# Which engine forms the second parts of the weights outside the middle of the MLP

## The chip, the cores and the metric

The kernel runs on one core of a Trainium2 chip. Its engines are named as the profile names them: PE is TensorE with the matmuls, PEld its loading of weights, DVE is VectorE, ACT is ScalarE, POOL is GpSimd and SP is SyncE, which issues most transfers. The metric is the device time of one execution in microseconds (us); the median of several executions is compared.

## What is computed

Two layers of an encoder over 256 tokens of width 1024, in float32. Each layer does, in short:

```python
h = rmsnorm(x, norm_mix_pre)
proj = h @ w_in                      # q, k, v of A; pool input; q, k, v of C; three gates
ya = global attention, 8 heads       # branch A
yb = centred average pooling, minus identity, mapped by w_pool   # branch B
yc = neighbourhood attention         # branch C
merged = sum(sigmoid(gate_i + b_i) * (y_i @ w_branch[i]) for i in range(3))
x = x + rmsnorm(merged @ w_out, norm_mix_post)
h = rmsnorm(x, norm_ffn_pre)
up = conv over 3 tokens(h @ w_up)    # 2 x 2816 columns: val and gate
x = x + rmsnorm((gelu(gate) * val) @ w_down, norm_ffn_post)
```

## The kernel before

All weights come as one list of 264 chunks of 128 x 1024 float32 numbers (`CHUNKS`), 132 for each layer, in the order in which TensorE takes them. In one layer these are the first columns of w_in (24 chunks), then in six steps of gates and branches two chunks of w_branch and four of w_in each (with the first of w_out's eight in the last step), the rest of w_out, eight chunks of w_up for the first four blocks of 128 columns of both halves, and then pieces of w_up (two chunks each) with one chunk of w_down behind each from the sixth on. The last six chunks of w_down (`TAIL_D`) and the last five of w_out (`TAIL_O`) are tails of their own.

Each weight is used as a sum of two parts. For half a chunk (512 columns) ScalarE copies `raw` to `hi` in the type fp32r, and then the second part is formed, `lo` = `raw` - `hi`. Each product is three matmuls (lines 196 to 198): hi with hi, hi with lo and lo with hi. Activations are split the same way (`split_from`, lines 203 to 207), by ScalarE and VectorE.

The function `split(c, h)` does this for half h of chunk c, and line 160 chooses the engine of the second part. Of every five chunks the one with `c % PN == 1` (PN is 5) goes to GpSimd, with an exception: the chunks of w_in ahead of column 2816, where the gates begin. All others go to VectorE. The chunks run ahead of TensorE: up to six are split before they are used (NSPL), in six buffers each of `hi` and `lo`, and five `raw` buffers are loaded ahead (NRAW). `feed` calls `split` at a priority that is 100 behind the place in the program (LATER), while what stands in `urgent()` is 400 ahead. A scheduler turns the priorities into one fixed order for each engine when the kernel is built; each engine then runs its own list in order, and waits where an operand is missing.

Where one part of a layer ends and the next begins (`boundary`), the 256 tokens are taken as two halves t of 128. `tail` multiplies the last chunks for t = 0 first and then for t = 1. As soon as the banks of a half are done, `residual` forms the norm of them: squares on ScalarE (line 223), their sum on VectorE (line 225), the power -0.5 on GpSimd (`st`, line 215), two products with the gain on VectorE (`big`, line 259) and two with the norm, added to x (line 262). `norm_h` does the same for the next norm of x: lines 223, 225 and 215 and two products `xn` (`big`, line 242). TensorE then turns these (line 247), and the turned tile is split into `hThi` on ScalarE (line 203) and `hTlo` on VectorE (line 204). The next weights are multiplied with it, again for t = 0 first. Behind w_out this is `turned`: six chunks of w_up for t = 0, then the rest of the norm of t = 1, then these chunks for t = 1. There are three such boundaries: behind w_out in either layer, and behind w_down in the first.

GpSimd does little else: the powers of line 215, parts of the rotation of branch A (line 372), the rotation's tables, and the DMAs of line 638.

Of the kernel before, what the change touches and what calls it, by code (L numbers as in the profile page):

```python
# [21 lines left out]
NF = 22  # L22
EPS = 1e-6
CH = 1024
PN, LATER = 5, 100
NRAW, NSPL = 5, 6
NY = 20
TAIL_O, TAIL_D, LAG = 5, 6, 5
# [6 lines left out]
def chunk_list():  # L35

    out = []
    for l in range(L):
        def wide(name, i, c0, n):
            per = CH // n  # L40
            for k in range(0, 8, per):
                out.append((name, l, i, k, per, c0, n))
        wide("w_in", 0, 512, 256)
        wide("w_in", 0, 0, 512)
        for f in range(4):
            wide("w_in", 0, 768 + 128 * f, 128)
        for f in range(8):
            wide("w_in", 0, 1280 + 128 * f, 128)
        wide("w_in", 0, 2304, 512)
        for i in (1, 0, 2):  # L50
            for c in range(2):
                for k in (0, 2):
                    out.append(("w_branch", l, i, k, 2, 512 * c, 512))
                if i == 2 and c == 1:
                    out.append(("w_out", l, 0, 0, 1, 0, 1024))
                wide("w_in", 0, 2816 + 1024 * i + 512 * c, 512)
        for d in range(1, 8 - TAIL_O):
            out.append(("w_out", l, 0, d, 1, 0, 1024))
        for d in range(8 - TAIL_O, 8):
            out.append(("w_out", l, 0, d, 1, 0, 1024))  # L60
        wide("w_up", 0, 0, 128 * NT)
        wide("w_up", 0, 128 * NF, 128 * NT)
        for f in range(NT, NF):
            wide("w_up", 0, 128 * f, 128)
            wide("w_up", 0, 128 * (NF + f), 128)
            if 0 <= f - LAG < NF - TAIL_D:
                out.append(("w_down", l, 0, f - LAG, 1, 0, 1024))
        for f in range(NF - TAIL_D, NF):
            out.append(("w_down", l, 0, f, 1, 0, 1024))
    return out  # L70


CHUNKS = chunk_list()
# [3 lines left out]
def encoder(ctx: ExitStack, tc: tile.TileContext, x, norms, wall, bgate, gqk, wpool, pscale,  # L77
# [66 lines left out]
    def feed_dma(upto=len(CHUNKS)):  # L144
        while cur["dma"] < upto and cur["dma"] < cur["lo"] + NRAW:
            c = cur["dma"]
            raw[c] = sb.tile([128, CH], FT, name="raw", bufs=NRAW)
            nc.sync.dma_start(raw[c], wall[c])
            cur["dma"] += 1

    def split(c, h):

        if h == 0:
            hi[c] = sb.tile([128, CH], FR, name="hi", bufs=NSPL)
            lo[c] = sb.tile([128, CH], FR, name="lo", bufs=NSPL)
        z = slice(h * CH // 2, (h + 1) * CH // 2)
        act.activation(hi[c][:, z], raw[c][:, z], AF.Copy)  # L157

        lean = c % PN == 1 and (CHUNKS[c][0] != "w_in" or CHUNKS[c][5] >= 2816)
        (pool if lean else dve).tensor_tensor(lo[c][:, z], raw[c][:, z], hi[c][:, z], op=OP.subtract)  # L160
        if h == 1:
            del raw[c]
            cur["lo"] += 1
            feed_dma()

    def feed(upto=len(CHUNKS)):

        at = tc.cur_priority
        tc.cur_priority = at + LATER
        while cur["lo"] < upto and cur["lo"] < min(cur["used"] + NSPL, cur["dma"]):  # L170
            c = cur["lo"]
            for h in range(2):
                split(c, h)
        tc.cur_priority = at
# [152 lines left out]
    with tc.issue_after(par["xn"].ins):  # L327
        split(0, 0)
    drive(entry[0])
    with tc.issue_after(par["hi"].ins), tc.issue_after(par["lo"].ins):  # L330
        split(0, 1)
# [8 lines left out]
    for l in range(L):  # L340
# [468 lines left out]
        for f in range(NT, NF):  # L809
# [3 lines left out]
            if f < 2 * NT:  # L813
                q = psbank()
                for z in range(2):
                    for t in range(2):
                        c = 512 * z + 128 * (f - NT)
# [105 lines left out]
```

## Time and profile before

| what | value |
|---|---|
| median of 3 runs | 837.64 us (836.85 to 838.1) |
| the profiled execution | 837.28 us, of which its span is 835.5 us |
| PE busy | 806.2 us |
| DVE busy | 597.0 us |
| ACT busy | 501.7 us |
| POOL busy | 182.5 us |
| second parts on DVE | 440, 307.0 us |
| second parts on POOL | 88, 122.7 us |

The rest of the profiled execution's time, 1.8 us, lies around its span. The busy times are those of one execution and of the whole span. Stages have different limits, so a change in one stage is read from that stage. An engine's idle time that is shown before an instruction is what it stood still, with the instruction or transfer that it waited for behind the arrow.

### The profile page before, as it was taken

The page shows a single profiled execution, that of the slowest core. Times are in us where ns is not written, and L with a number is a line of the kernel's source. Part 1 is how long each engine was busy: PE and PEld are TensorE (multiplying, and loading weights), DVE is VectorE, ACT ScalarE, POOL GpSimd, SP SyncE. Part 2 cuts the span into 40 slices and gives each one's busy share as a digit, 9 for nine tenths or more (in the row PEclk, how much of TensorE's full clock was granted, in tenths as well). Part 3 has the DMA queues.
Part 4 walks back from the last instruction along what each step waited for, and adds up shares of the span by engine and source line. Part 5 has one row for each costly group of instructions (what it writes and reads, how often), then busy time and mean ns, then how long its engine had stood idle before and what let it go on. Part 6 is the DMA issues. An engine that isn't in the chain of part 4 may idle for free.

```text
span 835.5 us, 13700 instructions
## 1 busy us (share of the span) xinstructions
PE 806.2 (96%) x5012; PEld 707.2 (85%) x5012; DVE 597.0 (71%) x1101; ACT 501.7 (60%) x1068; POOL 182.5 (22%) x183
## 2 busy tenths in 40 slices
PE   4989999999999999999999899999998999999997
PEld 4888788888779999999889887888887899999995
DVE  4799475676677976766689964777667598667664
ACT  5478565455658756566565865654545677565661
POOL 2421422122122111212122015112212211212120
PEclk9999999999999999999999999999999999999999
DMA  7947557655565765565355545456654655556531
GB/s 269 336 159 217 164 176 230 199 183 170 193 218 183 206 195 182 185 191 182 124 199 175 176 155 153 164 181 205 230 179 139 209 175 195 186 184 184 192 101 50
DMA packets 44867, 154.42 MB, mean 185 GB/s; under 512 B 6017, under 2 KB 6273, under 8 KB 44545
## 3 DMA queue, kind: packets, MB, share of 16 engines
q1 hardware_dynamic: 43776, 151.46, 55.9%
q0 software_dynamic: 1024, 2.10, 0.9%
q8 instruction: 39, 0.64, 0.3%
q14 instruction: 28, 0.22, 0.1%
HBM read 150.39 MB, written 1.05 MB: 181 GB/s over the span
## 4 chain that ended last, share of the span: by engine, by line
PE 81%; DVE 10%; issue 2%; ACT 2%; POOL 2%; DMA 1%; SPq 0%; DVEq 0%; POOLq 0%; ACTq 0%
PE ps L196 26%; PE ps L197 25%; PE ps L198 25%; DVE lo L160 3%; POOL st L215 2%; DVE big L242 1%; DMA x<-in_x 1%; DVE big L379 1%; PE ps L481 1%; ACT hi L157 1%; PE ps L471 1%; DVE x L262 1%; PE ps L530 1%; PE ps L497 1%; PE ps L596 0%
## 5 line engine op out<-in xcount | busy, mean ns | idle before, releaser
L157 ACT ACTIVATE hi<-raw 128x512 fp32r<-128x512 f32 x528 | 310.9, 624 | 115.3 <-PE ps L197 40.1
L160 DVE TENSOR_TENSOR lo<-raw,hi 128x512 fp32r<-128x512 f32 x440 | 307.0, 723 | 72.9 <-ACT hi L157 71.0
L160 POOL TENSOR_TENSOR lo<-raw,hi 128x512 fp32r<-128x512 f32 x88 | 122.7, 1414 | 510.4 <-ACT hi L157 499.7
L196 PE MATMUL ps<-hThi,hi 128*128 128x256 f32 x768 | 219.0, 285 | 0.0
L198 PE MATMUL ps<-hThi,lo 128*128 128x256 f32 x768 | 218.1, 284 | 0.0
L197 PE MATMUL ps<-hTlo,hi 128*128 128x256 f32 x768 | 217.9, 284 | 0.0
L196 PEld LDWEIGHTS ps<-hThi,hi 128*128 128x128 f32 x768 | 147.9, 193 | 2.2 <-issue 0.8
L197 PEld LDWEIGHTS ps<-hTlo,hi 128*128 128x128 f32 x768 | 147.9, 193 | 1.4
L198 PEld LDWEIGHTS ps<-hThi,lo 128*128 128x128 f32 x768 | 147.8, 192 | 0.1
L196 PE MATMUL ps<-hi,hThi 128*128 128x512 f32 (+1 forms) x352 | 136.0, 388 | 1.2 <-ACT hi L157 0.9
L198 PE MATMUL ps<-hi,hTlo 128*128 128x512 f32 (+1 forms) x352 | 134.4, 382 | 0.9 <-DVE hTlo L204 0.9
L197 PE MATMUL ps<-lo,hThi 128*128 128x512 f32 (+1 forms) x352 | 134.6, 383 | 0.3 <-DVE lo L160 0.2
L196 PE MATMUL ps<-hi,y 128*128 128x512 f32 x272 | 107.3, 394 | 0.0
L197 PE MATMUL ps<-lo,y 128*128 128x512 f32 x272 | 106.4, 391 | 0.0
L198 PE MATMUL ps<-hi,y 128*128 128x512 f32 x272 | 105.9, 389 | 0.0
L196 PEld LDWEIGHTS ps<-hi,hThi 128*128 128x128 f32 x352 | 66.4, 189 | 15.4 <-ACT hi L157 1.1
L198 PEld LDWEIGHTS ps<-hi,hTlo 128*128 128x128 f32 x352 | 66.4, 189 | 14.6 <-DVE hTlo L204 2.3
L197 PEld LDWEIGHTS ps<-lo,hThi 128*128 128x128 f32 x352 | 66.4, 189 | 14.1 <-DVE lo L160 2.1
L799 ACT ACTIVATE w<-ps,cvp 128x256 f32<-128x256 f32 x88 | 48.3, 557 | 35.0 <-DVE w L801 35.0
L800 DVE SCALAR_TENSOR_TENSOR w<-ps,cvp,w 128x255 f32<-128x255 f32 x88 | 41.8, 480 | 28.6 <-ACT w L799 28.5
L196 PEld LDWEIGHTS ps<-hi,y 128*128 128x128 f32 x272 | 51.2, 188 | 11.0 <-issue 1.1
L198 PEld LDWEIGHTS ps<-hi,y 128*128 128x128 f32 x272 | 51.1, 188 | 11.0
(121 smaller groups left out, 843.0 us busy)
## 6 DMA issues: line engine op xcount, KB each, us to landing
raw<-in_wall SPq DMA_DIRECT2D x264, 512.0 KB, 4.1
gb<-in_bgate SPq DMA_DIRECT2D x12, 256.0 KB, 5.0
gpre<-in_norms SPq DMA_DIRECT2D x4, 512.0 KB, 6.1
rpbt<-in_rpbt SPq DMA_DIRECT2D x2, 1024.0 KB, 7.3
gpost<-in_norms SPq DMA_DIRECT2D x4, 512.0 KB, 4.8
vb<-w POOLq DMA_DIRECT2D x32, 64.0 KB, 2.6
x<-in_x SPq DMA_DIRECT2D x4, 256.0 KB, 6.4
out_x<-x SPq DMA_DIRECT2D x4, 256.0 KB, 2.0
```

The costliest lines, as they stand in the source:

```text
L157: act.activation(hi[c][:, z], raw[c][:, z], AF.Copy)
L160: (pool if lean else dve).tensor_tensor(lo[c][:, z], raw[c][:, z], hi[c][:, z], op=OP.subtract)
L196: pe.matmul(o, a[0], b[0], start=first, stop=False)
L197: pe.matmul(o, a[0], b[1], start=False, stop=False)
L198: pe.matmul(o, a[1], b[0], start=False, stop=last)
L215: pool.tensor_tensor(r, v, mhalf[:, :width], op=OP.pow)
L242: par["xn"] = dve.scalar_tensor_tensor(xn[:, c], xs[t][:, c], r, g[:, c], op0=OP.mult, op1=OP.mult)
L262: dve.scalar_tensor_tensor(xs[t][:, c], mg[:, c], r, xs[t][:, c], op0=OP.mult, op1=OP.add)
L379: dve.tensor_tensor(o5[:, :, :, b], v5[:, :, :, 1 - b], t5[:, None, :, b].to_broadcast([128, n, 2, 16]), op=OP.mult)
L471: pe.transpose(p3[:, k, t * 128:(t + 1) * 128], e[:, t, k * 128:(k + 1) * 128], ident)
L799: act.activation(u[:, c:c + S], p[:, c:c + S], AF.Identity, bias=cvp[:, l, j, 3:4], scale=cvp[:, l, j, 1:2])
L800: dve.scalar_tensor_tensor(u[:, c + 1:c + S], p[:, c:c + S - 1], cvp[:, l, j, 0:1], u[:, c + 1:c + S], op0=OP.mult, op1=OP.add)
```

## The change

It changes the condition in `split` alone. Before, GpSimd forms the second part of each chunk with `c % 5 == 1`, from the gates of each layer on. After, it does so only if the chunk also belongs to one of the single pieces of w_up (`CHUNKS[c][6] == 128`, the fifth block on) or to w_down ahead of its tail. In all other stages VectorE forms the second parts of every chunk: in the gates, the branches, w_out, the first four blocks of w_up and the tail of w_down. The order of the chunks, the number of buffers and the priorities stay.

```diff
@@ -156,7 +156,9 @@
         z = slice(h * CH // 2, (h + 1) * CH // 2)
         act.activation(hi[c][:, z], raw[c][:, z], AF.Copy)
 
-        lean = c % PN == 1 and (CHUNKS[c][0] != "w_in" or CHUNKS[c][5] >= 2816)
+
+        name, f = CHUNKS[c][0], CHUNKS[c][3]
+        lean = c % PN == 1 and (name == "w_up" and CHUNKS[c][6] == 128 or name == "w_down" and f < NF - TAIL_D)
         (pool if lean else dve).tensor_tensor(lo[c][:, z], raw[c][:, z], hi[c][:, z], op=OP.subtract)
         if h == 1:
             del raw[c]
```

A chunk's entry holds name, layer, index, first block of 128 rows, blocks, first column and columns, so `CHUNKS[c][3]` is the block of rows (of w_down: the block f that it multiplies), `[5]` the first column and `[6]` the columns of a block.

## Rows read from the trace of the kernel before

**Rows 1.** The page's first part: busy time, share of the span and instructions.

```profile
PE 806.2 (96%) x5012; PEld 707.2 (85%) x5012; DVE 597.0 (71%) x1101; ACT 501.7 (60%) x1068; POOL 182.5 (22%) x183
```

**Rows 2.** Busy time by stretches: stretch, its length, each engine's busy time, granted clock, DMA.

```profile
92.00:220.00 128.00, 127.62 (x685) 103.72 (x684) 81.03 (x151) 68.50 (x146) 34.60 (x34) 1.00 0.62 199
492.00:628.00 136.00, 135.62 (x728) 109.95 (x727) 87.25 (x161) 73.35 (x157) 35.27 (x34) 1.00 0.57 185
220.00:245.00 25.00, 23.38 (x105) 17.59 (x104) 20.01 (x31) 15.29 (x35) 6.12 (x6) 1.00 0.45 152
628.00:652.00 24.00, 21.66 (x101) 17.00 (x100) 18.10 (x28) 13.45 (x31) 6.02 (x6) 1.00 0.43 136
415.00:432.00 17.00, 16.36 (x93) 13.78 (x92) 15.20 (x28) 11.50 (x29) 2.49 (x3) 1.00 0.63 210
390.00:405.00 15.00, 15.00 (x111) 14.28 (x110) 10.19 (x19) 9.35 (x20) 3.27 (x3) 1.00 0.60 189
```

**Rows 3.** Second parts by group (busy us, mean ns), and who waited for them.

```profile
L160 DVE TENSOR_TENSOR lo<-raw,hi 128x512 fp32r<-128x512 f32 x440 | 307.0, 723 | 72.9 <-ACT hi L157 71.0
...
PE ps L197 <- DVE lo L160: 0.2, 1, 0.2
```

**Rows 4.** POOL's timeline at the two changes from w_out to the MLP: start, length.

```profile
230.87 1.81 POOL L160 TENSOR_TENSOR lo<-raw,hi 128x512 fp32r<-128x512 f32 x1 [0.57 <-ACT hi L157]
...
235.53 1.27 POOL L160 TENSOR_TENSOR lo<-raw,hi 128x512 fp32r<-128x512 f32 x1
...
635.63 2.96 POOL L160 TENSOR_TENSOR lo<-raw,hi 128x512 fp32r<-128x512 f32 x2
```

**Rows 5.** DVE's timeline at the same places: the residual's and the norm's products.

```profile
226.33 1.41 DVE L242 SCALAR_TENSOR_TENSOR big<-x,st,gpre 128x512 f32<-128x512 f32 x2 [0.46 <-POOL st L215]
...
230.78 2.45 DVE L262 SCALAR_TENSOR_TENSOR x<-big,st,x 128x512 f32<-128x512 f32 x2
...
235.59 2.42 DVE L242 SCALAR_TENSOR_TENSOR big<-x,st,gpre 128x512 f32<-128x512 f32 x2 [0.45 <-POOL st L215]
...
635.64 3.50 DVE L242 SCALAR_TENSOR_TENSOR big<-x,st,gpre 128x512 f32<-128x512 f32 x2 [0.45 <-POOL st L215]
```

**Rows 6.** PE's timeline at the three boundaries; in brackets the idle time and its releaser.

```profile
227.14 0.66 PE L247 MATMUL ps<-ident,big 128*128 128x128 f32 x4 [0.22 <-DVE big L242]
...
235.54 0.39 PE L198 MATMUL ps<-hi,hTlo 128*128 128x512 f32 x1
235.77 0.40 PE L196 MATMUL ps<-hi,hThi 128*128 128x512 f32 x1
237.41 1.21 PE L247 MATMUL ps<-ident,big 128*128 128x128 f32 x7 [1.24 <-DVE big L242]
...
421.96 0.39 PE L198 MATMUL ps<-hi,hTlo 128*128 128x256 f32 x1 [0.47 <-DVE hTlo L204]
...
637.51 0.66 PE L247 MATMUL ps<-ident,big 128*128 128x128 f32 x4 [1.29 <-DVE big L242]
...
639.29 0.63 PE L247 MATMUL ps<-ident,big 128*128 128x128 f32 x4 [0.42 <-DVE big L242]
...
641.00 0.50 PE L198 MATMUL ps<-hi,hTlo 128*128 128x512 f32 x1 [0.38 <-DVE hTlo L204]
```

**Rows 7.** DVE's second parts at the third boundary (a row of the timeline, the group), and 628 to 652.

```profile
418.82 1.89 DVE L160 TENSOR_TENSOR lo<-raw,hi 128x512 fp32r<-128x512 f32 x3
...
L160 DVE TENSOR_TENSOR lo<-raw,hi 128x512 fp32r<-128x512 f32 x12 | 7.8, 682 | 0.0
...
L160 DVE TENSOR_TENSOR lo<-raw,hi 128x512 fp32r<-128x512 f32 x8 | 5.3, 684 | 0.0
```

**Rows 8.** DVE's waits for `hi` (us in total, times, longest), and two later stretches.

```profile
DVE lo L160 <- ACT hi L157: 71.0, 74, 3.7
...
458.00:463.00 5.00, 1.65 (x12) 1.27 (x11) 4.89 (x8) 2.40 (x7) 0.00 (x0) 1.00 0.89 304
463.00:467.00 4.00, 4.00 (x23) 4.00 (x22) 3.91 (x9) 3.92 (x7) 0.00 (x0) 0.57 0.03 11
```

## The prediction

> **What bounds the kernel now.** I read four views, from coarse to fine. First the page's line of busy shares [rows 1]: TensorE is busy for 806.2 of 835.5 us, so at most some 29 us can be won at all, and only where TensorE stands still. Second the busy time by stretches [rows 2], to see where that is. The gates, branches and w_out of each layer (92 to 220 us and 492 to 628 us), where most of the moved work lies, leave TensorE idle for 0.38 us each (128.00 - 127.62, and 136.00 - 135.62). The two changes from w_out to the MLP (220 to 245, 628 to 652) leave 1.62 and 2.34 us. The change from the first layer's MLP to the second layer (415 to 432) runs the same code, `boundary`, and leaves 0.64 us. So the change's worth is read at the two changes from w_out to the MLP, and the third is my measure of how they look when GpSimd forms no weights: no second part runs on it there.
>
> Third, the timelines of GpSimd and VectorE there. In each of the two stretches GpSimd forms the two pieces of one chunk [rows 4]: at 230.87 and 235.53 in the first layer (chunk 71), and from 635.63 in the second (chunk 201). These fall on the norm's own work on VectorE: a pair of products of the norm and the residual takes 1.41 us at 226.33, with GpSimd still, but 2.45 us at 230.78, 2.42 us at 235.59 and 3.50 us at 635.64 [rows 5]. All of them read both tensors from SBUF, as the pieces on GpSimd do. The extensions are 1.04 + 1.01 = 2.05 us in the first layer and 2.09 us in the second.
>
> Fourth, TensorE's timeline, to see whether these reach it. They do: it waits for exactly those products (`big` of line 242) with 1.24 us before 237.41, and with 1.29 and 0.42 us before 637.51 and 639.29; then 0.38 us at 641.00 for `hTlo`, which VectorE forms next [rows 6]. An idle time shown is less than what is lost: from 235.77 to 237.41 are 1.64 us, of which one step of 512 columns takes 0.23 (235.54 to 235.77), so 1.41 us are lost where 1.24 is shown. I add 0.17 us for each such wait.
>
> **The change part by part.** The lists of chunks and the two conditions give 44 chunks on GpSimd before and 21 after; none is added. 23 chunks, 46 instructions of 128x512, go to VectorE: 13 of the gates and branches (7 in the first layer, 6 in the second), 4 of w_out, 3 of the first four blocks of w_up, and 3 of the tails of w_down (chunks 126 and 131 in the first layer, 261 in the second).
>
> *Their price on VectorE.* Three pieces in a row take 1.89 us at 418.82 [rows 7], 0.60 us apart, so 46 cost 27.6 us of VectorE. Their average of 723 ns [rows 3] includes the extension by GpSimd. Part of the 27.6 comes back, since the 46 pieces that leave GpSimd no longer stretch others.
>
> *Gates, branches, w_out body.* VectorE is busy for 81.03 of 128 us and 87.25 of 136 us there [rows 2]. Even with all of the added work (some 18 pieces, 10.8 us, each) it stays near 72%. In the whole run TensorE waited for a second part on VectorE once, 0.2 us [rows 3], with chunks up to six ahead. I cost these parts at nothing; the cover is this lead and TensorE's own work. Were it gone, each late piece would cost 0.6 us. A gain here is excluded but for the 0.38 us of idle time, which ends on ScalarE's `vb` and not on a second part.
>
> *Tails of w_down.* Two chunks of the first layer and one of the second. VectorE gets 1.2 us per chunk beside the conv pieces. TensorE is busy for all of the 15 us from 390 to 405, in which VectorE has 4.81 us to spare [rows 2]; I take nothing, with one late piece, 0.6 us, as the bound against it, and no gain, since nothing waits there.
>
> *The first layer's boundary* (chunk 71). Both extended pairs become 1.41 us. TensorE's idle time of 1.62 us then keeps the 0.22 us before 227.14 [rows 6], which comes before GpSimd's pieces start and so stays. Gain: 1.40 + 0.17 = 1.57 us.
>
> *The second layer's boundary* (chunk 201). The 1.29 us shrinks to the 0.22 us of the first layer's same place, the 0.42 us goes, and the 0.38 us for `hTlo` grows to the 0.47 us seen before 421.96 in the third boundary, where three second parts stand in VectorE's queue between the norm and `hTlo` [rows 6, 7]. So 2.09 + 3 x 0.17 = 2.60 us become 0.22 + 0.47 + 2 x 0.17 = 1.03. Gain: 1.57 us.
>
> Sum: 3.14 us. The profiled execution took 837.28 us, 835.5 of them span; 837.28 - 3.14 = 834.1. The median of the runs shown is 0.36 us above that execution, so I forecast 834.5.
>
> *Bounds.* The four moved pieces of these boundaries cost at most 4 x 0.60 = 2.4 us, if all stand in the chain that TensorE waits for, against 2.05 + 2.09 = 4.14 us of extension returned: 1.7 us at least, 4.1 us at most if they fit wholly into VectorE's waits for `st` (0.45 us at 235.59 and 635.64). I take a value between, nearer the upper end, since the third boundary holds 12 second parts on VectorE and still loses only 0.64 us. Its tail of w_down, though, covers the first norm by six chunks rather than five, which is why I keep the 0.22 us.
>
> The Trainium skill ("SBUF — State Buffer", "Who interferes with whom") calls the ports that VectorE and GpSimd share an exclusive lock: a VectorE instruction with two SBUF inputs against a GpSimd one that reads SBUF, and the loser waits for the whole instruction. By that each of the four pieces could return its full 1.27 us (the one at 235.53), 5.1 us together, where the rows show 4.14; I keep the rows.
>
> **The rivals.**
>
> *The added pieces take the place of the contention.* For: VectorE is busy for 20.01 of 25 us in the first boundary [rows 2], executes in order, and each piece ahead of the norm delays it by 0.60 us. If further pieces are drawn forward in its queue as well (some three in each boundary), the 4.14 us are eaten: 4.14 - 2.4 - 1.2 = 0.5 us, 837.1. Against: the third boundary. The Trainium skill ("Perfetto Trace Analysis", "Optimizing Scalar/DVE Operations") says that where VectorE is saturated, moving work away from it, to GpSimd even, may make sense, though the shared port may spoil that; this change goes the other way, and by the first half of the sentence would not gain. The rows bear out the second half.
>
> *Waits for the first part stand in VectorE's queue: slower.* On GpSimd a piece waits for ScalarE's `hi` and holds up only GpSimd. On VectorE everything behind it waits too: it lost 71.0 us over 74 such waits, at most 3.7 us in one [rows 8]. If the scheduler puts a moved piece with such a longest wait ahead of the norm in both boundaries, 2 x 3.7 + 4 x 0.6 - 4.14 = 5.7 us are added: 843.3. It decides from a wait of 0.9 us each (2 x 0.9 + 2.4 = 4.2). A stop of TensorE can cost more: after 3.35 us of idleness between 458 and 463 its clock was granted at 0.57 over the next 4 us [rows 8], part of them at 1.2 rather than 2.4 GHz. Against: the second parts on VectorE in the second layer's and the third boundary show no idle time before them now [rows 7].
>
> *The waits are hidden anyway.* Another wait ends just behind the norm (`hTlo` on ScalarE's `hThi`, weights of the chunk itself), and only a part of the 3.14 us shows. With half, 836.1: still no measurable change. The idle of 0.64 us in the third boundary speaks against it.
>
> **How the numbers follow.** What this kernel's measurement tells from no change is about 0.2%, 1.7 us. The forecast case (gain 1.7 to 4.1 us) has 0.66; a larger gain, by a luckier order of the queues, 0.03; the place of the contention taken, or the gain hidden, 0.20 together; the slower rival 0.11. So faster 0.69, same 0.20, slower 0.11. The likeliest case's own range is 833.5 (837.64 - 4.14) to 835.9. The 8 in 10 reach 0.6 us further down, for the spread of the runs, to 832.9, and up through most of the hidden cases to 837.2; left out are the slower rival, the last of the hidden cases and the largest gains.
>
> **What would show it.** Right: in both boundaries no GpSimd second part; pairs of lines 242 and 262 at 1.4 us throughout; TensorE's idle time down to 0.3 to 0.7 us in the first and 0.9 to 1.1 us in the second; busy time of TensorE unchanged, and the span 3 us shorter; VectorE's busy time up by less than 27.6 us. Wrong, if TensorE newly waits in the gates or tails for `lo` on VectorE, if the waits before line 247 remain with VectorE's second parts standing before line 242 or 262, or if VectorE idles on `hi` there. The forecast would also fail if the changed queue moves the entry of the second layer (458 to 467), which loses 3.35 us and a stretch of clock now.

## The result, and the profile after

The changed kernel takes 833.27 us in the median of 6 runs (832.17 to 833.65), the kernel before 837.41 us in the median of 6 (836.6 to 838.1): a ratio of 0.995, 95% interval 0.994 to 0.996, faster by 4.1 us. The forecast was 834.5, with a range of 832.9 to 837.2. The profiled execution took 833.36 us, 831.5 of them span. In the changed kernel's code all lines behind 160 stand two further down: the second parts are line 162, the matmuls 198 to 200, the residual's product with the norm 264, the norm's 244, the turning 249.

The page's first part, with the two groups of second parts from its fifth:

```profile
PE 807.5 (97%) x5012; PEld 709.7 (85%) x5012; DVE 602.5 (72%) x1147; ACT 501.7 (60%) x1068; POOL 115.7 (14%) x137
...
L162 DVE TENSOR_TENSOR lo<-raw,hi 128x512 fp32r<-128x512 f32 x486 | 323.7, 693 | 81.3 <-ACT hi L157 78.9
...
L162 POOL TENSOR_TENSOR lo<-raw,hi 128x512 fp32r<-128x512 f32 x42 | 56.0, 1354 | 237.0 <-ACT hi L157 236.1
```

GpSimd lost 46 pieces and 66.8 us of busy time, and VectorE, which took them, is busy for only 5.5 us more (597.0 to 602.5). Its second parts fell from 723 to 693 ns on average [rows 3].

The busy times by stretches, as in [rows 2] (the second boundary comes some 3 us earlier now):

```profile
92.00:220.00 128.00, 127.62 (x682) 103.62 (x681) 84.81 (x170) 67.65 (x146) 8.84 (x16) 1.00 0.62 200
492.00:628.00 136.00, 135.62 (x724) 109.90 (x723) 89.02 (x179) 72.48 (x157) 8.71 (x16) 1.00 0.56 182
220.00:245.00 25.00, 24.72 (x114) 19.45 (x113) 20.78 (x37) 17.70 (x38) 3.05 (x4) 1.00 0.52 173
625.00:649.00 24.00, 23.72 (x110) 18.62 (x109) 18.30 (x32) 14.98 (x34) 3.06 (x4) 1.00 0.46 151
```

In the gates and branches nothing changed for TensorE: 0.38 us idle in each layer, as before. In the two changes from w_out to the MLP its idle time fell from 1.62 and 2.34 us to 0.28 and 0.28 us. VectorE's timeline there shows why, with the rows that answer to [rows 5]:

```profile
225.48 1.42 DVE L244 SCALAR_TENSOR_TENSOR big<-x,st,gpre 128x512 f32<-128x512 f32 x2 [0.45 <-POOL st L217]
226.82 0.69 DVE L162 TENSOR_TENSOR lo<-raw,hi 128x512 fp32r<-128x512 f32 x1
...
229.93 1.41 DVE L264 SCALAR_TENSOR_TENSOR x<-big,st,x 128x512 f32<-128x512 f32 x2
...
233.71 1.42 DVE L244 SCALAR_TENSOR_TENSOR big<-x,st,gpre 128x512 f32<-128x512 f32 x2 [0.44 <-POOL st L217]
235.05 1.29 DVE L162 TENSOR_TENSOR lo<-raw,hi 128x512 fp32r<-128x512 f32 x2
...
633.30 1.42 DVE L244 SCALAR_TENSOR_TENSOR big<-x,st,gpre 128x512 f32<-128x512 f32 x2 [0.45 <-POOL st L217]
634.63 0.68 DVE L162 TENSOR_TENSOR lo<-raw,hi 128x512 fp32r<-128x512 f32 x1
```

Each pair of products takes 1.41 or 1.42 us, where three of them took 2.42 to 3.50. The added second parts do not stand ahead of the norm: behind the second norm there are two in a row (235.05) where there was one. TensorE's timeline, which answers to [rows 6], has one wait of 0.23 us left in each boundary, and the transposes for the second half of the tokens come without one:

```profile
226.29 0.66 PE L249 MATMUL ps<-ident,big 128*128 128x128 f32 x4 [0.23 <-DVE big L244]
...
234.56 1.17 PE L249 MATMUL ps<-ident,big 128*128 128x128 f32 x7
...
634.10 0.66 PE L249 MATMUL ps<-ident,big 128*128 128x128 f32 x4 [0.23 <-DVE big L244]
...
642.38 1.15 PE L249 MATMUL ps<-ident,big 128*128 128x128 f32 x7
```

From the first of these groups to the second are 8.27 us in the first layer; before, 227.14 to 237.41, they were 10.27.

To see where time goes over the whole span I set the start of each of TensorE's matmuls against that of the same matmul of the other kernel. In these two profiles the changed kernel is 0.86 us ahead at 17 us, before any instruction that the change touches; 2.88 ahead behind the first boundary; it loses 0.54 at the entry of the second layer; and goes from 2.34 to 4.36 ahead at the second boundary. Everywhere else nothing moves by more than 0.1 us. Each boundary gave 2.02 us. The 0.86 at the start and the 0.54 at the entry are what single profiles of all the kernels below differ by there, too.

### The profile page after: what moved, and what is told of

Same layout as the page of the kernel before. It is cut to its first block, busy times and chain, and to the rows that moved or that the text cites. A ratio compares the mean times of both kernels' runs of the same rounds, so it can differ in the third digit from the quotient of the medians.

```text
span 831.5 us, 13689 instructions
## 1 busy us (share of the span) xinstructions
PE 807.5 (97%) x5012; PEld 709.7 (85%) x5012; DVE 602.5 (72%) x1147; ACT 501.7 (60%) x1068; POOL 115.7 (14%) x137
## 4 chain that ended last, share of the span: by engine, by line
PE 82%; DVE 10%; issue 3%; POOL 2%; ACT 2%; DMA 1%; SPq 0%; DVEq 0%; POOLq 0%; ACTq 0%
PE ps L198 26%; PE ps L199 25%; PE ps L200 25%; DVE lo L162 3%; POOL st L217 2%; DMA x<-in_x 1%; DVE big L244 1%; DVE big L381 1%; PE ps L483 1%; DVE x L264 1%; PE ps L473 1%; ACT hi L157 1%; PE ps L532 1%; PE ps L499 1%; DVE hTlo L206 1%
## 5 line engine op out<-in xcount | busy, mean ns | idle before, releaser
L162 DVE TENSOR_TENSOR lo<-raw,hi 128x512 fp32r<-128x512 f32 x486 | 323.7, 693 | 81.3 <-ACT hi L157 78.9
L162 POOL TENSOR_TENSOR lo<-raw,hi 128x512 fp32r<-128x512 f32 x42 | 56.0, 1354 | 237.0 <-ACT hi L157 236.1
L217 POOL TENSOR_TENSOR st<-st,mhalf 128x1 f32<-128x1 f32 (+1 forms) x20 | 20.3, 1013 | 364.4 <-DVE st L227 342.2
L198 PEld LDWEIGHTS ps<-hi,y 128*128 128x128 f32 x272 | 51.2, 188 | 11.0 <-issue 1.1
```

The costliest lines, as they stand in the source:

```text
L198: pe.matmul(o, a[0], b[0], start=first, stop=False)
L217: pool.tensor_tensor(r, v, mhalf[:, :width], op=OP.pow)
```

## The experiments

Each was timed beside the kernel before, on the same chip; "gained" and "lost" are again the starts of the same matmuls of two profiles, in us.

**e1_only_two: two of the 23 chunks.** The kernel before, and in it:

```diff
+        lean = lean and c not in (71, 201)
```

> The kernel before, with chunks 71 and 201 alone given to VectorE (4 of the 46 pieces). Theory A (GpSimd's pieces stretch the norm's products on VectorE in the two changes from w_out to the MLP, and that is the whole gain): both boundaries lose 2.0 us less, and the time is that of the changed kernel, 833.3 us, 4.0 below before; elsewhere no matmul moves by more than 0.1 us. Rival B (the gain is spread over the 46 pieces, since VectorE and GpSimd disturb each other everywhere): 4 of 46 of it, 0.4 us, 837.0.

833.9 us against 837.32, ratio 0.9961 (0.9947 to 0.9976). Against before, the first boundary gained 2.03 us and the second 2.01, and nothing moved in between but the stretch at the entry of the second layer. VectorE's busy time fell, from 597.0 to 595.1 us, though it has four pieces more. The chunks 71 and 201 are the change, as far as time goes.

**e2_all_but_two: the other 21.** The changed kernel, and in it:

```diff
+        lean = lean or c in (71, 201)
```

> The changed kernel, with chunks 71 and 201 given back to GpSimd, so 42 of the 46 pieces are moved. Theory A: the gain is gone, 837.4 us within 0.8; the pairs of products of the norm there take 2.4 to 3.5 us again in place of 1.4. Rival B: most of the gain stays, 833.7. Rival C (the added work on VectorE delays something in the gates and branches, and the two boundaries pay for more than the sum): above 838.

838.06 us against 837.32, ratio 1.001 (1.0001 to 1.002). VectorE's timeline has the stretched pairs back, at the same three places:

```profile
231.56 2.45 DVE L265 SCALAR_TENSOR_TENSOR x<-big,st,x 128x512 f32<-128x512 f32 x2
...
236.38 2.42 DVE L245 SCALAR_TENSOR_TENSOR big<-x,st,gpre 128x512 f32<-128x512 f32 x2 [0.44 <-POOL st L218]
...
636.46 3.46 DVE L245 SCALAR_TENSOR_TENSOR big<-x,st,gpre 128x512 f32<-128x512 f32 x2 [0.45 <-POOL st L218]
```

Against before, no matmul behind 25 us moved by more than 0.1 us, but at the entry of the second layer for some 4 us. The 0.7 us by which this run is later stand ahead of 25 us, where both kernels do the same; I did not find their cause. So rival C, which would begin above 838, has no place where it could have paid, and moving 42 pieces to VectorE is worth nothing.

**e3_reads: the reads land elsewhere.** The changed kernel, with two products on GpSimd in `norm_h`, for the first half of the tokens behind w_out (the lines that pass on `extra` and the tile are left out here):

```diff
             r = rms(halves(xs[t]))
+            if extra:
+                for h in range(2):
+                    pool.tensor_tensor(par["spare"], xs[t][:, :512], g[:, :512], op=OP.add)
```

Their result, written to the dead table of branch C, is read by nothing.

> The changed kernel, with two products of GpSimd added behind the norm's power for the first half of the tokens in both changes from w_out to the MLP; they read two SBUF tiles of 128x512 and write a tile that is read by nothing, so no weight comes from GpSimd. Theory A in its strict form (the reading of GpSimd stretches VectorE's products that read two SBUF tiles): the pair of line 242's products there takes 3.5 us in place of 1.42 and each boundary loses 2.0 us, 837.3 us together. Rival D (in the kernel before TensorE waited because GpSimd delivers a weight's second part late, 1.3 us where VectorE takes 0.6): no weight is late here, so no loss, 833.3.

838.04 us, ratio 1.0011 (1.0002 to 1.002), as theory A says, but by way of other instructions. GpSimd's timeline, then VectorE's second parts at this place in the changed kernel and here:

```profile
223.29 3.45 POOL L243 TENSOR_TENSOR rpbt<-x,gpre 128x512 f32<-128x512 f32 x2 [0.86 <-DVE x L267]
227.49 0.94 POOL L217 TENSOR_TENSOR st<-st,mhalf 128x1 f32<-128x1 f32 x1 [0.75 <-DVE st L227]
```

```profile
222.94 1.29 DVE L162 TENSOR_TENSOR lo<-raw,hi 128x512 fp32r<-128x512 f32 x2
```

```profile
223.79 3.50 DVE L162 TENSOR_TENSOR lo<-raw,hi 128x512 fp32r<-128x512 f32 x2
```

The scheduler put the products ahead of the norm's power `st`, and so beside two second parts on VectorE, which read two SBUF tiles each as well. These took 3.50 us in place of 1.29. The sum of line 227 stands behind them in VectorE's queue, and the power waited for that sum: GpSimd had ended its products and stood still for 0.75 us before 227.49. Line 247's pair then took 1.42 us. Each boundary lost 2.1 us, to the same stretching as before, but of two instructions that stand earlier in VectorE's queue than those that the theory had named. No weight came late from GpSimd, so this already speaks against rival D.

**e4_writes and e5_reads_behind: writing against reading.** The same place, with GpSimd's added work held behind the power: five writes of a constant in e4, the two products in e5 (only the added work is shown).

```diff
+            if extra:
+                with tc.issue_after(par["rstd"].ins):
+                    for h in range(5):                                   # e4
+                        pool.memset(par["spare"], 0.0)
+                    for h in range(2):                                   # e5, in its place
+                        pool.tensor_tensor(par["spare"], xs[t][:, :512], g[:, :512], op=OP.add)
```

> As the run with added reads, but GpSimd writes the same tile five times with a constant (it reads nothing; one such write of 128x512 took 0.53 us in the kernel before, so five about the time of the two products). Theory A strict: no product on VectorE is stretched, 1.42 us for the pair, 833.3 us. Rival E (any work of GpSimd beside VectorE stretches it): as with the reads, up to 2.0 us in each boundary, 837.3.

> The run with added reads again, but with GpSimd's two products held behind the norm's power in its queue (in the first such run they stood ahead of it). Theory A strict (GpSimd's reads of SBUF stretch VectorE's products that read two SBUF tiles): line 242's pair takes 3.5 us in place of 1.42, TensorE's first wait for it grows by 1.1 us and a second appears, each boundary loses 2.0 us against the changed kernel: 837.3 us. Rival D (a late second part was the cause in the kernel before): no loss, 833.3.

With the writes the time is 832.49 us, ratio 0.9948 (0.9933 to 0.9963), and neither boundary gained or lost 0.1 us against the changed kernel. GpSimd's and VectorE's timelines:

```profile
225.43 2.85 POOL L244 MEMSET rpbt<- 128x512 f32 x5
```

```profile
225.51 1.41 DVE L248 SCALAR_TENSOR_TENSOR big<-x,st,gpre 128x512 f32<-128x512 f32 x2 [0.45 <-POOL st L217]
```

With the reads it is 837.51 us, ratio 1.0002 (0.9993 to 1.0011): the gain is gone, with every weight's second part where the changed kernel has it. Each boundary lost 2.06 us. The same timelines, and TensorE's:

```profile
226.04 2.96 POOL L244 TENSOR_TENSOR rpbt<-x,gpre 128x512 f32<-128x512 f32 x2
```

```profile
226.09 3.46 DVE L248 SCALAR_TENSOR_TENSOR big<-x,st,gpre 128x512 f32<-128x512 f32 x2 [0.45 <-POOL st L217]
```

```profile
227.91 0.66 PE L253 MATMUL ps<-ident,big 128*128 128x128 f32 x4 [1.24 <-DVE big L248]
229.69 0.63 PE L253 MATMUL ps<-ident,big 128*128 128x128 f32 x4 [0.43 <-DVE big L248]
231.40 0.50 PE L200 MATMUL ps<-hi,hTlo 128*128 128x512 f32 x1 [0.39 <-DVE hTlo L206]
```

These are the second layer's waits of [rows 6] (1.29, 0.42, 0.38) over again, in the first layer and without a weight from GpSimd. So the cause is GpSimd's reading beside VectorE's products of two SBUF tiles, and a late second part (rival D) is excluded. 2.85 us of writes over the same pair cost nothing, so rival E falls. The Trainium skill ("SBUF — State Buffer", "Who interferes with whom") says just this of a VectorE instruction with two SBUF inputs: it contends with GpSimd where that reads SBUF, not where it only writes; the two runs agree, 3.46 us against 1.41.

**e6_all_dve: no second part on GpSimd at all.**

```diff
+        lean = False
```

> The changed kernel with the other 42 pieces on VectorE too, so that GpSimd forms no second part at all. Theory A: in the middle of the MLP the pieces on GpSimd stretch the conv's products of two SBUF tiles (lines 204 and 805), so moving them costs VectorE less than 42 x 0.60 = 25.2 us, some 10 us net, beside TensorE at 100%: no change, 833.3 us within 0.8. Rival F (there VectorE needs the help: it is busy for 72% and its chain of conv pieces feeds w_down): TensorE starts to wait in the MLP, slower than the changed kernel by 1 us or more.

833.37 us, ratio 0.995 (0.9933 to 0.9967): the changed kernel's time. In the middle of the MLP VectorE's stretch in the changed kernel and here (the first row and the second):

```profile
285.00:395.00 110.00, 110.00 (x778) 103.62 (x778) 78.79 (x145) 66.44 (x131) 18.77 (x14) 1.00 0.58 187
```

```profile
285.00:395.00 110.00, 110.00 (x779) 103.71 (x778) 82.18 (x160) 66.87 (x132) 0.00 (x0) 1.00 0.59 189
```

TensorE is full in both. VectorE's whole busy time rises by 10.7 us (602.5 to 613.2) for 42 pieces that cost 25.2 us at 0.60: even there GpSimd's help is worth less than half of what it takes over. Rival F falls.

**e7_entry: more for GpSimd, where VectorE is fullest.**

```diff
+        lean = lean or c in (6, 11, 16, 21, 136, 141, 146, 151)
```

> The changed kernel with 8 more chunks given to GpSimd, 16 pieces at the entries of both layers (chunks 6, 11, 16, 21, 136, 141, 146, 151), where VectorE is the fullest engine (98% in 458 to 463 us of the kernel before) and TensorE waits for it. Theory A (a piece on GpSimd saves VectorE 0.60 us but stretches its products of two SBUF tiles by up to 1.1 us): no gain, and up to 2 us lost in each entry, 833.3 to 837. Rival G (where VectorE is full any work taken off it helps): 16 x 0.60 = 9.6 us less on VectorE, TensorE's waits of 2.5 us at the first and 3.3 us at the second entry shrink by half, 830.5.

839.81 us, ratio 1.0031 (1.0022 to 1.0041): 6.5 us slower than the changed kernel and 2.6 slower than before. The first entry lost 4.0 us, and the third boundary with the second entry 1.3. VectorE's second parts from 20 to 70 us, in the changed kernel and here, and what TensorE waited for here:

```profile
L162 DVE TENSOR_TENSOR lo<-raw,hi 128x512 fp32r<-128x512 f32 x33 | 21.8, 701 | 0.0
```

```profile
L163 DVE TENSOR_TENSOR lo<-raw,hi 128x512 fp32r<-128x512 f32 x25 | 21.2, 877 | 1.3 <-ACT hi L157 1.2
```

```profile
PE ps L474 <- DVE w L466: 3.6, 1, 3.6
```

With 8 pieces fewer in that window VectorE is busy with second parts for 0.6 us less, not 4.8: the others grew from 701 to 877 ns. Rival G falls, and the size of theory A was too small at the first entry (up to 2 us expected). A part of the rest may be the clock: from 60 to 70 us it was granted at 0.83, and at 1.00 in the changed kernel. The Trainium skill ("Perfetto Trace Analysis", "Optimizing Scalar/DVE Operations") allows for offloading a saturated VectorE to GpSimd and warns that the shared port may spoil it; here the warning is what came true.

**e8_entry_order and e9_entry_order2: the order at the entries.** e7 showed the entries to be sensitive. In the changed kernel seven second parts stand in VectorE's queue ahead of `klo` at the second entry, 4.31 us, while TensorE waits. e8 forms weights ahead later there; e9 leaves out only the third block's turn. The line that puts the last second part of q into `par["q"]` is left out here.

```diff
             if f == P1:
                 drive(preps[1])
-            feed()
+                with tc.issue_after(par["q"].ins):      # VectorE's last second part of q
+                    feed()
+            elif f not in (1, 2):                       # e9: (2,)
+                feed()
```

> The changed kernel with another order at the two entries: the forming of weights ahead is left out behind the second and third pool block and made up for behind the fourth, after VectorE's last second part of q (issued behind it). VectorE's queue then holds four second parts of weights, not seven, ahead of klo of the second half of the tokens. Theory H (the queue of second parts of weights on VectorE, 4.3 us long, is what TensorE waits for there): the wait of 1.4 us for klo goes and the 1.9 us behind it shrinks, with it the stretch at half clock: 1.5 to 3 us less at each entry, 827 to 830.5. Rival I (ScalarE's copies in the chain, one after the other, are what ends last): less than 0.5 us for each entry, 832.5 or more. Rival J (the weights come late instead): TensorE waits for lo or hi, 833.3 or more.

> The same with the forming left out behind the third pool block only, so that the weights keep a longer lead; VectorE's queue there is between the two others. Theory H: between the changed kernel and the other run, 829 to 832. Rival I: 832.5 or more. Rival J: better than the other run.

834.31 us, ratio 0.9967 (0.9957 to 0.9977), and 834.75, ratio 0.9966 (0.9953 to 0.9979): both no better than the changed kernel. But the parts differ. In e8 the second entry gained 2.4 us and the first lost 1.5, with this wait of TensorE at the first that the changed kernel has not:

```profile
PE ps L200 <- DVE lo L162: 3.0, 1, 3.0
```

In e9 they gained 1.8 and lost 1.7; at its first entry TensorE waits not for `lo` but for `w` of line 465, 2.4 us where the changed kernel has 1.4. So theory H holds at the second entry; at the first the put-off second parts come late (rival J, in e8) or hold up `w` (in e9).

**e10_second_entry: the same in the second layer alone.** The lines of e8, with `l > 0` as a further condition.

> The changed kernel with the other order at the entry of the second layer alone. In the run with it at both entries TensorE gained 4.3 us at the second (waits of 3.3 us and the stretch at half clock down to 0.5 us and none) and lost 1.5 us at the first, where second parts of weights came 3.0 us late. Theory H: 833.3 - 4.3 = 829.0 us, 8 below the kernel before. Rival K (the gain at the second entry in that run came from its later arrival there): less than half of it, 831.5 or more.

831.17 us in five runs (830.25 to 832.03), ratio 0.9933 to before (0.992 to 0.9947). It is faster than the kernel before by 6 us. Its ratio is lower than the changed kernel's 0.995 (0.994 to 0.996), though the two intervals just overlap. At the entry it gained 2.5 us over the changed kernel, not 4.3. Two stretches of the entry in the changed kernel and in this one:

```profile
454.00:459.00 5.00, 2.12 (x16) 1.72 (x14) 4.92 (x9) 2.75 (x8) 0.00 (x0) 0.96 0.91 267
459.00:465.00 6.00, 5.53 (x26) 5.56 (x27) 5.88 (x12) 5.46 (x11) 0.00 (x0) 0.50 0.19 76
```

```profile
454.00:459.00 5.00, 4.51 (x36) 4.11 (x35) 4.81 (x8) 4.61 (x11) 0.00 (x0) 1.00 0.41 126
459.00:465.00 6.00, 4.43 (x33) 3.86 (x32) 5.97 (x15) 3.86 (x9) 0.00 (x0) 1.00 0.18 44
```

TensorE's long stop and the stretch at a granted clock of 0.50, that is 1.2 GHz, behind it are gone. By 466.02 of the changed kernel's time this had brought 4.7 us; at 468.65, behind the next step of the chain, 2.5 of them are left:

```profile
465.81 0.63 PE L473 MATMUL ps<-ident,w 128*128 128x128 f32 x4 [1.70 <-DVE w L465]
```

VectorE's softmax scaling (`w`) is late now, behind the second parts that were put off. e8 has the same wait of 1.7 us there, and the 4.3 us of the expectation above were read on matmuls ahead of it, at 468.2 of the changed kernel's time. Counted behind it, e8 gained 2.4 us, about as much as e10, though it came to the entry 2.8 us later. So the later arrival (rival K) is not the cause, and theory H holds with a smaller price than 4.3 us.

## Why the prediction was right

*What bounds the kernel.* Right: the gain lies in the two boundaries and nowhere else (e1, e2), TensorE had no new wait in the gates, branches, w_out or tails, and its 0.38 us there stayed.

*The mechanism.* Right: the pieces on GpSimd stretched VectorE's products, TensorE waited for them, and both ended with the change. The prediction read it from the timelines; e3, e4 and e5 show it.

*The sum.* 3.14 us were forecast, 1.57 for each boundary; each gave 2.02. The mis-sized terms are two. For the second layer I let `hTlo`'s wait grow from 0.38 to 0.47 us, with three second parts between the norm and `hTlo` as in the third boundary. There is one (634.63), as in the kernel before (639.06), and the wait is gone. By the starts of the matmuls the three waits gave 1.06, 0.59 and 0.43 us; the first two are as forecast, and for the third I had counted a loss of 0.09. A wait of 0.25 us for `hThi`, before 649.92 in the kernel before, went too and brought nothing: the matmuls are 4.43 us ahead at 641.00 and 4.36 at 658.66.

For the first layer the long wait gave the 1.41 us that I had counted. But TensorE had also waited, before it, for second parts that stood behind the stretched residual pair in VectorE's queue, and these waits gave 0.55 us more, where 0.16 of shown idle time was all that I had left for them. In the kernel before, TensorE's loading of weights:

```profile
233.88 0.19 PEld L197 LDWEIGHTS ps<-lo,hThi 128*128 128x128 f32 x1 [0.52 <-DVE lo L160]
...
235.20 0.19 PEld L197 LDWEIGHTS ps<-lo,hThi 128*128 128x128 f32 x1 [0.33 <-DVE lo L160]
```

Together the four moved pieces cost the chain nothing, where I had bounded them by 2.4 us: 4.04 us gained of the 4.14 that the stretched pairs could give back, which was the upper bound. So the time, 833.27 us, lies not in the likeliest case's own range (833.5 to 835.9) but 0.2 us under it, since the kernel before took 837.41 us beside it and not the 837.64 from which that range was worked out.

*VectorE's load.* Forecast as less than 27.6 us; measured 5.5, so some four fifths of the work that GpSimd had done for VectorE it had also cost VectorE.

*The rivals.* That the added pieces eat the gain did not come: they stand behind the norm. That they wait for `hi` in VectorE's queue did not come either; its waits for `hi` grew from 71.0 to 78.9 us over the whole span without TensorE waiting for one more. That another wait hides the gain is excluded by the 0.28 us left. The entry of the second layer, named as what could break the forecast, moved by 0.54 us.

## What to carry to other kernels

A second engine is no free hand if its reads hold up the first, as here: count what its work takes from the first, on each of the first's operations that reads two SBUF tiles, before counting what it takes over. Here two chunks of 44 decided the time, since theirs fell on the one chain that TensorE waited for; look where the borrowed work lands, not how much it is. Put off work to shorten one queue only after looking at who waits for it next.

## What the runs showed of the hardware

Two GpSimd products of 128x512 that read SBUF lengthen a pair of VectorE's products by 2.04 us (1.42 to 3.46) and take 2.96 us themselves, while five writes of the same tile, 2.85 us, lengthen it by nothing. On the other hand two VectorE operations that read one tile from PSUM were not stretched by GpSimd's products. In the kernel before, GpSimd alone and then from 617.76 us, and VectorE beside the latter:

```profile
214.37 2.54 POOL L160 TENSOR_TENSOR lo<-raw,hi 128x512 fp32r<-128x512 f32 x2 [6.51 <-ACT hi L157]
...
617.76 3.13 POOL L160 TENSOR_TENSOR lo<-raw,hi 128x512 fp32r<-128x512 f32 x2 [12.43 <-ACT hi L157]
```

```profile
617.80 0.68 DVE L160 TENSOR_TENSOR lo<-raw,hi 128x512 fp32r<-128x512 f32 x1
618.40 0.68 DVE L207 SCALAR_TENSOR_TENSOR ck<-ps,vb 128x512 fp32r<-128x512 f32 x1
619.00 0.68 DVE L674 SCALAR_TENSOR_TENSOR w<-w,ps 128x512 f32<-128x512 f32 x1
619.71 1.73 DVE L675 TENSOR_TENSOR q<-q,w 128x512 f32<-128x512 f32 x1
```

The second and third read one tile from PSUM and take their usual 0.68 us; the last reads both from SBUF and takes 1.73. The first reads both from SBUF too and was not stretched, while GpSimd's pair took 0.59 us longer than at 214.37. So it seems that there GpSimd was the one that waited; the rows do not show why.

In the changed kernel TensorE stood still for 2.88 of the 5 us from 454 us, and the 6 us behind them had a granted clock of 0.50. In e10 it stood still for 0.49 of these 5 us, and the clock stayed at 1.00. That the slow stretch goes with the stop I had seen as a risk and not as something to win.
